# Linear attention on one core: a store that waits for the load six octets ahead through a dependency, with eight output buffers

## The chip, the cores and the metric

The kernel runs on one core of one Trainium2 chip. The metric is the device time of one execution in microseconds (us). Three runs of the kernel before the change gave 126.98, 126.65 and 126.52 us, a median of 126.65 us.

## The reference

The kernel computes linear attention with a ReLU feature map, for 8 batches of 12 heads, 512 rows of sequence and 64 columns, everything in float32 in HBM:

```python
Q_feat = np.maximum(0, Q)
K_feat = np.maximum(0, K)
KV = np.einsum('bhkd,bhkv->bhdv', K_feat, V)
K_sum = np.sum(K_feat, axis=2)
numerator = np.einsum('bhqd,bhdv->bhqv', Q_feat, KV)
denominator = np.einsum('bhqd,bhd->bhq', Q_feat, K_sum)
return numerator / (denominator[:, :, :, None] + 1e-10)
```

Q, K, V and the output have 8 x 12 x 512 x 64 float32 elements each, 12.58 MB.

## The kernel before

The 96 heads are cut into 12 **octets** of 8 heads (the variable `o`, from 0 to `NO - 1` = 11), and each octet into two **groups** of 4 heads (`g` = 2o and 2o + 1). A group of K or of V is 0.52 MB in HBM; the Q of an octet and the output of an octet are 1.05 MB each. An octet therefore reads 3.15 MB and writes 1.05 MB.

**Loads.** Only the four loads of octet 0's K and V go through the queues of SP and ACT, as float32 (lines 103 to 107). All others are issued by GpSimd (POOL) in one fixed order and turn float32 into bf16 on the way (`load_kv`, lines 94 and 96, and `load_q`, line 100): for each octet K, V, K, V, Q. They land in rings of 12 K tiles, 12 V tiles and 7 Q tiles, so loads run octets ahead of the arithmetic. POOL does nothing else of weight.

**Arithmetic.** The program order of the engines is written out by hand (a manual schedule; lines 254 to 328). For an octet, DVE and ACT apply the ReLU to K and spread K and V into block layouts (`prep` line 136 and 138, `prep_v` lines 143 and 145). PE accumulates KV in PSUM (`mm_kv`, line 150), ACT copies it out (`evac_kv`, line 160). PE transposes Q (`transp`, line 171), ACT applies the ReLU (line 179). PE forms the denominators (line 210) and the transposed outputs (line 201), ACT copies those out (line 203), PE turns them back (`back`, line 228), and DVE multiplies by the reciprocal denominators into the output tile `o_sb` (`norm`, line 234). In the main loop octet o's arithmetic goes with the conversion of octet o + 1's K and V, and the outputs of octet o - 1 are finished there (`backs(o - 1)`); the last four octets have an order of their own.

**Stores.** The output tiles come from the pool `outp` (line 51, `DELAY + 2` = 7 buffers of 8 KB per partition). Two of its buffers first hold the float32 K and V of octet 0. `store(o, o_sb)` (lines 240 to 249) issues the store of octet o on the SP queue, which executes in order. Stores are held back on purpose: for the first seven octets SP first issues a copy of 128 bytes from the first K tile of octet o + 5 into `scratch` (line 242). That copy has to wait until this K tile has landed, and the store stands behind it in the same queue. Each copy also writes the same `scratch`, so it waits for the copy before it. Stores 7 to 11 have no such copy of their own; the last store is cut in two halves.

The lines that set it:

```python
DELAY = 5
outp = pool("outp", DELAY + 2)
if o + DELAY < NO:
    nc.sync.dma_start(out=scratch, in_=k_sb[2 * (o + DELAY)][0:1, 0, :])
```

Of the kernel before, what the change touches and what calls it, by code (L numbers as in the profile page):

```python
# [10 lines left out]
def kernel(  # L11
# [7 lines left out]
    nc = tc.nc  # L19
    B, H, S, D = Q.shape  # L20
# [10 lines left out]
    NG = NH // NHG  # L31
    NO = NG // 2
    assert NO * 8 == NH and R == 16 and RQ == 32
    DELAY = 5
    F32 = 2

    fp32 = mybir.dt.float32
    bf16 = mybir.dt.bfloat16
# [3 lines left out]
    def pool(name, bufs, **kw):  # L42
        return ctx.enter_context(tc.tile_pool(name=name, bufs=bufs, **kw))

    consts = pool("consts", 1)
# [4 lines left out]
    rcp = pool("rcp", 2)  # L50
    outp = pool("outp", DELAY + 2)
    otp = pool("otp", 2)
# [5 lines left out]
    def view(X, f):  # L58
        return X.rearrange("b h s d -> (b h s d)").rearrange("(n p f) -> n p f", p=P, f=f)

    Qr, Kr, Vr, Or = view(Q, RQ * D), view(K, R * D), view(V, R * D), view(out, RQ * D)
# [14 lines left out]
    kvf = [consts.tile([P, 8 * 2 * D1], bf16, name=f"kvd{i}") for i in range(NK)]  # L76
    kvd = [x.rearrange("p (h d) -> p h d", h=8) for x in kvf]
    mask = consts.tile([P, 2, 2], fp32, name="mask")
    scratch = consts.tile([1, D], bf16, name="scratch")

    mask_h = consts.tile([P, 8, 2], fp32, name="mask_h")

# [5 lines left out]
    ctx.enter_context(tc.manual_schedule())  # L88

    q_sb, k_sb, v_sb = {}, {}, {}  # L90

    def load_kv(g):
        k_sb[g] = kin.tile([P, R, D], bf16, name="k_sb")
        nc.gpsimd.dma_start(out=k_sb[g].rearrange("p r d -> p (r d)"), in_=Kr[g])  # L94
        v_sb[g] = vin.tile([P, R, D], bf16, name="v_sb")
        nc.gpsimd.dma_start(out=v_sb[g].rearrange("p r d -> p (r d)"), in_=Vr[g])  # L96

# [12 lines left out]
    for o in range(1, NO):  # L110
        load_kv(2 * o)
        load_kv(2 * o + 1)
        load_q(o)
# [124 lines left out]


    def store(o, o_sb):  # L240
        if o + DELAY < NO:
            nc.sync.dma_start(out=scratch, in_=k_sb[2 * (o + DELAY)][0:1, 0, :])
        Ov = Or[o].rearrange("p (r d) -> p r d", d=D)
        if o == NO - 1:
            for j in range(2):
                rs = slice(RQ // 2 * j, RQ // 2 * (j + 1))
                nc.sync.dma_start(out=Ov[:, rs], in_=o_sb[:, rs])
            return
        nc.sync.dma_start(out=Ov, in_=o_sb)

    def out_tile():
        return outp.tile([P, RQ, D], fp32, name="o_sb", tag="o_sb")
# [19 lines left out]
    def backs(o):  # L272
        o_sb = out_tile()
        for j in range(2):
            norm(o, j, back(o, j), o_sb)
        store(o, o_sb)
# [26 lines left out]
    o = NO - 2  # L303
    g = 2 * NO - 2
# [9 lines left out]
    o_sb = out_tile()  # L314
# [4 lines left out]
    for i in range(2):  # L319
        relu_q(o + 1, i, transp(o + 1, i), nc.vector if i == 1 else None)  # L320
    norm(o, 1, ps, o_sb)
    store(o, o_sb)
    idle(5, o + 1)
    out_t(o + 1, (0,))
# [32 lines left out]
```

## Time and profile before

| What | Value |
|---|---|
| median of three runs | 126.65 us (126.52 to 126.98) |
| span of the profiled execution, first to last instruction | 124.8 us |
| median less span | 1.85 us |
| PE, DVE, ACT busy | 69%, 65%, 64% of the span |
| HBM read, written | 37.75 MB, 12.58 MB |
| store issue to landing, median of 11 whole stores | 9.0 us |
| K, V, Q load issue to landing, medians | 14.1, 13.2, 14.8 us |
| 128-byte copy on SP, issue to landing, median of 7 | 5.0 us |

The profile gives the span of the execution that it recorded; a time of its own for that execution, with what lies around the span, is not given. The 1.85 us between the span and the median of the runs is therefore taken as fixed here. In the profile "DMA share" is the time that packets took, over 16 engines: 1.00 and above means that each of the 16 always had a packet in hand (packets of one engine can overlap, so it can pass 1). "GB/s" counts what was moved by packet size; a converting load counts with its bf16 size, half of what it read from HBM. For loads alone the HBM rate is thus twice the number shown.

### The profile page before, as it was taken

Reading aid. Unit: us, or ns where it says so; the run is one execution under the profiler, and the core shown is the slowest. Engines: PE = TensorE matmul, PEld = TensorE weight load, DVE = VectorE, ACT = ScalarE, POOL = GpSimd, SP = SyncE. Lnnn points to the kernel's source line nnn. Section 1 sums busy time; section 2 is a strip of 40 time slices with the busy share of each in tenths; the row PEclk is TensorE's granted clock in tenths of the full one; section 3 lists DMA queues with packets and bytes.
Section 4 is the critical chain, followed back from the end, with each engine's and each line's share of the span. In section 5 each row is a group of like instructions: output and inputs, shape, how many; then the busy total and the mean of one; then the engine's idle time right before and its main releaser. Section 6 shows DMA issues by size and latency. Waiting matters only on the chain.

```text
span 124.8 us, 2656 instructions
## 1 busy us (share of the span) xinstructions
PE 86.6 (69%) x1067; PEld 78.5 (63%) x1067; DVE 81.1 (65%) x176; ACT 79.4 (64%) x114; POOL 31.2 (25%) x62
## 2 busy tenths in 40 slices
PE   0032287998889899893598599399777577797600
PEld 0031285997878787792597499299576476695500
DVE  2257644759797997989147845934928918979430
ACT  0163369989898999988149558665939737737100
POOL 6902434314243331142133115034122000000000
PEclk9999999999999999999779859959999999999995
DMA  3999999999999999999999999999999999999993
GB/s 112 377 306 215 215 205 210 217 205 218 203 215 211 206 223 324 253 216 300 281 215 280 304 213 249 331 215 230 334 234 218 323 257 215 312 421 420 428 416 143
DMA packets 10748, 32.68 MB, mean 262 GB/s; under 512 B 1392, under 2 KB 1392, under 8 KB 9328
## 3 DMA queue, kind: packets, MB, share of 16 engines
q0 software_dynamic: 8064, 17.83, 74.7%
q1 hardware_dynamic: 2384, 13.63, 27.1%
q10 hardware_dynamic: 288, 1.05, 2.2%
q8 instruction: 8, 0.13, 0.4%
q14 instruction: 4, 0.03, 0.1%
HBM read 37.75 MB, written 12.58 MB: 403 GB/s over the span
## 4 chain that ended last, share of the span: by engine, by line
DMA 34%; DVE 30%; PE 23%; ACT 5%; issue 2%; DVEq 1%; SPq 0%; POOLq 0%; ACTq 0%
DMA v_sb<-in_V_dram 14%; DVE o_sb L234 13%; DMA q_sb<-in_Q_dram 13%; PE ps_kv L150 11%; DMA kv_first<-in_K_dram 7%; PE ps_bk L228 7%; DVE kf L136 5%; PE ps_qt L171 4%; DVE vo L138 3%; ACT kvd L160 2%; DVE vo L145 2%; PE ps_ot L201 2%; DVE den L218 2%; ACT qt L179 2%; DVE rec L222 1%
## 5 line engine op out<-in xcount | busy, mean ns | idle before, releaser
L150 PE MATMUL ps_kv<-vo,kf 128*128 128x132 bf16 x384 | 30.8, 244 | 17.7 <-ACT vo L143 8.2
L150 PEld LDWEIGHTS <-kf 128*128 128x128 bf16 x384 | 28.4, 110 | 19.0 <-DVE vo L138 10.9
L234 DVE TENSOR_TENSOR o_sb<-ps_bk,rec 128x1024 f32<-128x1024 f32 x24 | 28.3, 1219 | 17.1 <-PE ps_bk L228 17.1
L160 ACT CAST kvd<-ps_kv 64x260 bf16<-64x260 f32 (+1 forms) x54 | 18.7, 346 | 19.5 <-PE ps_kv L150 16.6
L203 ACT COPY ot_sb<-ps_ot 128x1024 f32<-128x1024 f32 x24 | 24.0, 1014 | 3.0 <-PE ps_ot L201 2.0
L179 ACT ACTIVATE qt<-ps_qt 128x1024 bf16<-128x1024 bf16 x23 | 22.4, 1026 | 5.6 <-PE ps_qt L171 5.5
L228 PE MATMUL ps_bk<-ident,ot_sb 128*128 128x128 f32 x192 | 23.0, 273 | 0.4 <-ACT ot_sb L203 0.4
L136 DVE TENSOR_SCALAR kf<-k_sb,mask 128x1024 bf16<-128x1024 bf16 x44 | 18.4, 460 | 6.4 <-DMA k_sb<-in_K_dram 6.3
L94 POOL DMA_DIRECT2D k_sb<-in_K_dram x22 | 11.9, 542 | 37.7 <-DMA q_sb<-in_Q_dram 24.1
L228 PEld LDWEIGHTS ps_bk<-ident,ot_sb 128*128 128x128 f32 x192 | 20.8, 141 | 0.7 <-ACT ot_sb L203 0.7
L171 PE MATMUL ps_qt<-ident,q_sb 128*128 128x128 bf16 x192 | 16.0, 250 | 6.0 <-DMA q_sb<-in_Q_dram 5.9
L171 PEld LDWEIGHTS <-q_sb 128*128 128x128 bf16 x192 | 14.3, 114 | 7.3 <-DMA q_sb<-in_Q_dram 7.1
L201 PE MATMUL ps_ot<-qt,kvd 128*128 128x256 bf16 x96 | 14.7, 283 | 5.0 <-DVE o_sb L234 4.3
L96 POOL DMA_DIRECT2D v_sb<-in_V_dram x22 | 12.3, 558 | 17.4 <-DMA k_sb<-in_K_dram 11.1
L201 PEld LDWEIGHTS <-kvd 128*128 128x128 bf16 x96 | 9.2, 101 | 7.8 <-issue 5.7
L138 DVE TENSOR_SCALAR vo<-v_sb,mask 128x1024 bf16<-128x1024 bf16 x22 | 10.6, 482 | 1.8 <-DMA v_sb<-in_V_dram 1.8
L143 ACT ACTIVATE vo<-v_sb,mask 128x1024 bf16<-128x1024 bf16 x10 | 11.5, 1152 | 0.2
L210 PEld LDWEIGHTS <-qt 128*128 128x128 bf16 x192 | 6.8, 97 | 4.4 <-ACT qt L179 3.4
L210 PE MATMUL ps_den<-kvd,qt 128*128 128x16 bf16 x192 | 7.5, 180 | 2.4 <-ACT qt L179 2.1
L100 POOL DMA_DIRECT2D q_sb<-in_Q_dram x12 | 6.6, 546 | 8.5 <-DMA v_sb<-in_V_dram 6.2
L213 DVE SCALAR_TENSOR_TENSOR own<-ps_den,mask_h 128x256 f32<-128x256 f32 x12 | 5.0, 417 | 3.3 <-PE ps_den L210 3.3
L136 DVE TENSOR_SCALAR kf<-kv_first,mask 128x1024 bf16<-128x1024 f32 x4 | 2.8, 749 | 5.1 <-DMA kv_first<-in_K_dram 5.1
(24 smaller groups left out, 28.3 us busy)
## 6 DMA issues: line engine op xcount, KB each, us to landing
out_dram<-o_sb SPq DMA_DIRECT2D x11, 1024.0 KB, 9.0
q_sb<-in_Q_dram POOLq DMA_DIRECT2D x12, 512.0 KB, 14.8
k_sb<-in_K_dram POOLq DMA_DIRECT2D x22, 256.0 KB, 14.1
v_sb<-in_V_dram POOLq DMA_DIRECT2D x22, 256.0 KB, 13.2
kv_first<-in_V_dram ACTq DMA_DIRECT2D x2, 512.0 KB, 7.2
kv_first<-in_K_dram SPq DMA_DIRECT2D x2, 512.0 KB, 6.9
out_dram<-o_sb SPq DMA_DIRECT2D x2, 512.0 KB, 4.3
scratch<-k_sb SPq DMA_DIRECT2D x7, 0.1 KB, 5.0
```

Source lines behind the costliest of these rows:

```text
L96: nc.gpsimd.dma_start(out=v_sb[g].rearrange("p r d -> p (r d)"), in_=Vr[g])
L136: nc.vector.tensor_scalar(kf[g][:, :, s, :], k_sb[g], scalar1=0.0, scalar2=mask[:, 0, s:s + 1], op0=Alu.max, op1=Alu.mult)
L138: nc.vector.tensor_scalar(vo[g % NB][:, :, 0, 2:D + 2], v_sb[g], scalar1=mask[:, 1, 0:1], scalar2=None, op0=Alu.mult)
L150: nc.tensor.matmul(ps_kv[:, g % 2, 0:2 * (D + 2)].rearrange("p (t d) -> p t d", t=2), kf[g][:, r, :, :].rearrange("p s d -> p (s d)"), vo[ ...
L160: copy(kvd[o % NK][64 * c:64 * c + 64, 4 * gs.start + s:4 * gs.stop:2, c * D1:c * D1 + D1].rearrange("p (g t) d -> p g t d", t=2), ps_kv[6 ...
L171: nc.tensor.transpose(ps[:, u, :], q_sb[o][:, i * (U // 2) + u, :], ident)
L179: nc.scalar.activation(to, ps, Act.Relu)
L201: nc.tensor.matmul(ps[:, i], kvd[o % NK][:, h, 1:2 * D + 1], q[:, :, h, :], start=True, stop=True, skip_group_check=True)
L203: nc.scalar.copy(ot[o][:, :, 4 * j:4 * j + 4], ps.rearrange("p h u c -> p u h c"))
L210: nc.tensor.matmul(ps[:, u], qt_sb[o % NZ][:, u, :], kvd[o % NK][:, :, 0:2 * D1:2 * D1 - 1], start=True, stop=True, skip_group_check=True)
L228: nc.tensor.transpose(ps[:, 2 * v:2 * v + 2].rearrange("p c d -> p (c d)"), ot[o][:, 8 * j + v].rearrange("p h c -> p (h c)"), ident32)
L234: nc.vector.tensor_tensor(o_sb[:, rs], ps, rec[o][:, rs].unsqueeze(2).to_broadcast([P, 16, D]), op=Alu.mult)
```

## The change

`DELAY` goes from 5 to 6, so the pool of output tiles has 8 buffers instead of 7, and the stores of octets 0 to 5 (before: 0 to 6) wait for the first K tile of the octet six later. The 128-byte copy and its `scratch` tile are gone. Instead `load_kv` keeps the instruction of each octet's first K load, and the store gets a dependency on that instruction. Order of loads, arithmetic and stores is the same.

```diff
-    DELAY = 5
+    DELAY = 6
...
-    scratch = consts.tile([1, D], bf16, name="scratch")
...
+    k_load = {}
+    after_load = mybir.DependencyInfo(mybir.DependencyClass.Sync, mybir.DependencyReason.DATA)
 
     def load_kv(g):
         k_sb[g] = kin.tile([P, R, D], bf16, name="k_sb")
-        nc.gpsimd.dma_start(out=k_sb[g].rearrange("p r d -> p (r d)"), in_=Kr[g])
+        ld = nc.gpsimd.dma_start(out=k_sb[g].rearrange("p r d -> p (r d)"), in_=Kr[g])
+        if g % 2 == 0:
+            k_load[g // 2] = ld
...
     def store(o, o_sb):
-        if o + DELAY < NO:
-            nc.sync.dma_start(out=scratch, in_=k_sb[2 * (o + DELAY)][0:1, 0, :])
         Ov = Or[o].rearrange("p (r d) -> p r d", d=D)
...
-        nc.sync.dma_start(out=Ov, in_=o_sb)
+        st = nc.sync.dma_start(out=Ov, in_=o_sb)
+        if o + DELAY < NO:
+            tc.add_manual_dep(st.ins, k_load[o + DELAY].ins.name, after_load, reason="store after load")
```

## The prediction

> **What bounds the kernel now.** I read the page's slices over time first, with the queue table under them, because the engines are busy only 64 to 69% of the span and the DMA row is not.
>
> ```profile
> DMA  3999999999999999999999999999999999999993
> GB/s 112 377 306 215 215 205 210 217 205 218 203 215 211 206 223 324 253 216 300 281 215 280 304 213 249 331 215 230 334 234 218 323 257 215 312 421 420 428 416 143
> ...
> q0 software_dynamic: 8064, 17.83, 74.7%
> q1 hardware_dynamic: 2384, 13.63, 27.1%
> ...
> HBM read 37.75 MB, written 12.58 MB: 403 GB/s over the span
> ```
>
> The DMA digit is 9 in every slice but the first and the last. Second view: the busy time by stretches, cut where the kind of traffic changes (loads alone to 42.85; loads with one store per octet to 102.85; then the tail; the last two columns are DMA share and GB/s).
>
> ```profile
> 12.00:42.85 30.85, 25.07 (x316) 22.94 (x317) 22.27 (x51) 24.78 (x39) 10.95 (x20) 1.00 1.10 210
> 42.85:102.85 60.00, 47.08 (x585) 42.95 (x585) 40.37 (x80) 42.12 (x59) 14.41 (x27) 0.91 1.09 263
> 102.85:110.00 7.15, 5.63 (x69) 5.04 (x67) 6.52 (x14) 5.31 (x10) 0.00 (x0) 1.00 1.09 279
> 110.00:118.00 8.00, 6.85 (x86) 5.79 (x84) 5.53 (x10) 3.59 (x5) 0.00 (x0) 1.00 1.01 424
> 118.00:122.00 4.00, 0.05 (x1) 0.00 (x0) 1.57 (x2) 0.00 (x0) 0.00 (x0) 1.00 1.00 415
> 122.00:123.60 1.60, 0.00 (x0) 0.00 (x0) 0.00 (x0) 0.00 (x0) 0.00 (x0) 0.59 0.51 207
> ```
>
> The share is 1.00 or more from 12 to 122 us: no DMA engine runs out of packets there. From 110 only stores move. The last 1.6 us are a drain at half share, and then about 1.2 us of closing waits end the span. Third view: SP's timeline, which shows the gate.
>
> ```profile
> 82.87 0.50 SPq L242 DMA_DIRECT2D scratch<-k_sb  x1
> ...
> 92.86 0.50 SPq L242 DMA_DIRECT2D scratch<-k_sb  x1
> 93.46 0.53 SPq L249 DMA_DIRECT2D out_dram<-o_sb  x1
> 102.85 0.50 SPq L242 DMA_DIRECT2D scratch<-k_sb  x1
> 103.45 11.23 SPq L249 DMA_DIRECT2D out_dram<-o_sb  x5
> 118.47 1.46 SPq L247 DMA_DIRECT2D out_dram<-o_sb  x2
> ```
>
> The gates open 10.0 us apart (42.90, 52.89, 62.89, 72.92, 82.87, 92.86, 102.85). One such period moves 3.15 MB of loads and 1.05 MB of store: 4.19 MB / 10.0 us = 419 GB/s. Loads alone run at 2 x 210 = 420 GB/s of HBM reads, stores alone at 424. So the three kinds of traffic cost the same per byte, and 50.3 MB / 0.42 = 119.8 us, which with some 3 us before the first data flow is the end of the transfers at 122 to 123.6. Last I read the chain of waits, which seems to say something else: its tail is arithmetic.
>
> ```profile
> 116.09 1.11 PE ps_bk L228 x8
> 117.19 0.02 issue
> 117.22 1.22 DVE o_sb L234
> 118.44 1.13 DVEq L352
> ```
>
> The chain follows engines and semaphores, and cannot see that a transfer queues behind older bytes. The two half stores issued at 118.47 and 119.6 land after 4.2 to 4.3 us. Half a megabyte at 0.42 MB/us takes 1.25 us; share 1.00 up to 122 says that the rest is at least partly queue. Both things end here almost together: the arithmetic hands over its last tile about when the queue of earlier stores has run down, and the bytes set the end.
>
> **The change part by part.**
>
> *One more store moves behind the loads.* Store 0 was released by octet 5's K (42.9). Octet 6's K landed at 52.89, with one store mixed in; without it an octet's loads take 3.15 / 0.420 = 7.5 us, so I expect the first gate at 42.9 + 7.5 = 50.4, then every 10.0 us, and the sixth and last (octet 11's K) at 100.4 instead of 102.85. All later loads come 2.5 us sooner, and store 6 joins the tail: after the last gate six whole stores and the two halves remain instead of five and the halves.
>
> *What the transfers' end does.* Bytes are the same. The moved store costs 10.0 - 7.49 = 2.51 us in the mixed phase and 1.05 / 0.424 = 2.47 us in the store phase: a gain of 0.04 us. Bounds: the slices with stores alone run from 416 to 428 GB/s, which makes the moved store 2.45 to 2.52 us, a gain of 0.06 or a loss of 0.01; I take 0.04, from the longest stretch.
>
> *What the arithmetic does.* It waited for loads in the middle: PE for Q at 60.77 (2.9 us), DVE for K at 62.90 (3.0 us) and 72.92 (1.65 us). With loads 2.5 us sooner these waits stay or just vanish, so the arithmetic's last multiply should move from 118.44 to about 116. Its price on the end is nothing, because the stores ahead of it in the queue then number one more: 2.5 us sooner in, 2.5 us more ahead. The cover is the store queue. If it were gone, the end would be issue plus service: 1.25 us for the data and what a lone transfer pays besides.
>
> *The drain.* In 122.0 to 123.6 the share is 0.51, so 0.49 x 1.6 = 0.78 us of 16 engines is lost. If that is starvation (the last halves arriving a little late at an almost empty queue), a longer queue regains up to 0.78 us. If the 16 engines just end their equal parts at unequal times, it regains nothing. The row nearest to it, 118 to 122 at share 1.00 with the first half issued at 118.47, shows no starvation, so I take 0 and keep 0.78 for the range.
>
> *The copies on SP.* Seven issues of 0.50 to 0.59 us go from SP. They lie in waits of up to 41 us, so they cost nothing; a store now starts 0.6 us sooner after its gate, again into a full queue. As transfers they are 7 x 128 bytes, under 0.001 MB. The wait for the copy before (24.9 us in total, six times) always ended before K came, since copies land in 5.0 us and gates are 10 us apart.
>
> *The wait on SP.* SP carries only stores after the first loads, so behind the waiting store 5 stand stores 6 to 11, and nobody waits for these but the closing waits and the output buffers. With 8 buffers, two of which hold octet 0's K and V first, octet 8 takes the buffer of store 0: landed by 50.4 + 13.2 (the longest landing) = 63.6, wanted after 90. For octets 9, 10 and 11 the distance stays above 20 us. POOL's queue is untouched: its loads are paced by older loads (24.1 us of waits on Q landings), and the rings of K, V and Q tiles are as before. One more store is outstanding after the last gate (5, 6, 7 and 8 at once and 9 soon after, instead of 6, 7, 8 and then 9 at 105.8); it could at worst block SP's issue, behind a queue that is full anyway.
>
> Sum: -0.04 + 0 + 0 = no change that can be measured; 126.65 - 0.04 rounds to 126.6. The profiled span of 124.8 should stay 124.8 (the 1.85 us around it fixed).
>
> A page against the trace: the 0.42 MB/us here stand above the per-core limit of about 358 GB/s that the Trainium skill gives in "DMA: Bandwidth & Descriptors", Specifications; by that figure alone 50.3 MB would need 141 us, more than the whole run, so here the measurement decides. The same table's fabric ceiling of 435 GB/s would put the transfers at an estimated 115.7 us, 4 us less than the 119.8 above; that would speak for a gain from any change that packs them better, but here loads alone, stores alone and both mixed stand at 420, 424 and 419, so I see nothing that this change packs. [...]
>
> **The rivals.**
>
> *A (forecast): the bytes set the end.* 126.6; own range 126.1 to 127.1.
>
> *B: the drain is starvation.* For it: the arithmetic hands over its last half at 119.6, with the queue nearly run down. Against: full share until 122. A deeper queue saves up to 0.78 us: 125.9. Faster by 0.6%.
>
> *C: the chain is right, the last tile sets the end.* Then the whole 2.5 us come off: 124.1 to 124.5. Against: for a store that has not been moved before the last load, its bytes are still to be moved after it, and the share of 1.00 leaves no hole to put them in; C needs engines that move 1.05 MB more than 420 GB/s allow.
>
> *D: the dependency is fulfilled by the issue of the K load and not its landing.* This is the case in which the change doesn't do what it says. Octet 6's K was issued at 38.25 and octet 11's at 85.90, so stores 0 to 8 would all be out when their tiles are ready (store 8's at about 97), three more than the six before 102.85. Three stores at 2.5 us push the last Q from 110 or a little before to 117.5; from the Q transposes (110.98) to the last multiply's end took 7.46 us, so 125, and a half store behind an empty queue 1.25 to 4.3 us more. End of landing 126.3 to 129.3 against 123.8: 129 to 132 us in all, 130.6 in the middle. It decides from where the last Q lands more than about 1 us later than before. For it: nothing in this trace shows how such an edge is turned into a wait. Against: an ordinary dependency on a K load makes DVE's conversion wait for the landing (6.3 us, three times, released by the DMA of K).
>
> **How the numbers follow.** Under 0.5%, 0.63 us, counts as no change for this kernel. A 0.78, B 0.11, C 0.03, D 0.05; 0.03 for slowdowns that I can't name. Faster: B and C, 0.14. Slower: 0.08. Same: 0.78. A holds 126.1 to 127.1 with most of its weight; to leave out no more than 2 in 10 the range goes down to B's full gain (125.8) and up to 127.2.
>
> **What would show it.** SP without copies, stores released near 50.4, 60.4, 70.4, 80.4, 90.4 and 100.4; a last multiply near 116; four stores issued one after the other from 100.4, a fifth near 103.3; DMA share 1.00 up to about 122, and store traffic alone from about 107.5. B is right if the drain becomes shorter than 1 us. D is right if the first store goes out at about 38. I am wrong if the rate of the stores alone falls with six queued, or if the share drops anywhere before 120.

## The result, and the profile after

The changed kernel takes 127.07 us (median of 8 runs, 126.93 to 127.15), the kernel before 126.68 us (8 runs, 126.52 to 126.98): a ratio of 1.0029, 95% interval 1.0019 to 1.0040. That is slower by 0.37 us, less than the 0.5% that I called no change, but clearly not zero, and I had forecast zero or a shade less. The profiled execution took 127.14 us with a span of 125.3 us; so 1.8 us lie around the span, as I had assumed, and the loss is inside it (124.8 before).

The first view is the page of the changed kernel, its slices and the queue of the stores:

```profile
DMA  3999999999999999999999999999999999999992
GB/s 101 380 305 215 216 207 211 214 207 217 210 209 210 209 218 204 216 305 277 212 286 301 210 259 329 209 236 333 228 218 324 256 212 317 400 424 429 424 405 86
...
q1 hardware_dynamic: 2160, 13.63, 26.7%
```

Queue q1 has the same bytes and 224 packets fewer: the 128-byte copies. The second view is its busy time by stretches, cut at the new gates (last two columns: DMA share and GB/s):

```profile
42.85:50.40 7.55, 6.79 (x100) 6.28 (x98) 6.60 (x15) 6.97 (x10) 2.71 (x5) 1.00 1.10 211
50.40:100.40 50.00, 37.73 (x466) 34.42 (x464) 32.36 (x63) 33.03 (x47) 12.03 (x22) 0.90 1.08 262
100.40:107.50 7.10, 5.58 (x73) 4.98 (x71) 5.57 (x11) 5.53 (x10) 0.00 (x0) 1.00 1.08 282
107.50:118.00 10.50, 7.86 (x95) 6.74 (x92) 8.03 (x13) 4.21 (x8) 0.00 (x0) 1.00 1.01 421
118.00:122.00 4.00, 0.00 (x0) 0.00 (x0) 0.03 (x1) 0.00 (x0) 0.00 (x0) 0.77 1.00 415
122.00:124.00 2.00, 0.00 (x0) 0.00 (x0) 0.00 (x0) 0.00 (x0) 0.00 (x0) 0.50 0.42 170
```

There is one more stretch of loads alone (to 50.4), then almost only stores from 107.5 (the last Q lands at 109.2), a full share to 122, and a drain as long as before. The third view is SP's timeline of the changed kernel, the first line of its stores and the two halves of the last:

```profile
50.41 62.72 SPq L250 DMA_DIRECT2D out_dram<-o_sb  x11
116.93 1.46 SPq L248 DMA_DIRECT2D out_dram<-o_sb  x2
```

The first gate at 50.4 and transfers that end where they did are what I forecast; the last store is issued 1.5 us sooner, where I had forecast about 2.5. The half stores land 5.8 to 5.9 us after issue instead of 4.2 to 4.3, so the last lands at 118.06 + 5.9 = 124.0 against 119.60 + 4.3 = 123.9.

What I had not looked at comes after the landing. At the end of the program SP goes through the program's semaphores in a fixed order, one instruction after the other. These are the instructions of that closing line, first of the kernel before in the window from 123.90 to 124.03 us, and then of the changed kernel in the window from 123.90 to 124.53 (duration min/median/max in ns, first and last start in us):

```profile
L352 SPq EVENT_SEMAPHORE  x1: 28/28/28, 123.9 to 123.9; - x1
L352 SPq DRAIN  x1: 7/7/7, 124.0 to 124.0; - x1
```

```profile
L355 SPq EVENT_SEMAPHORE  x8: 28/28/28, 124.0 to 124.4; - x8
L355 SPq DRAIN  x1: 7/7/7, 124.5 to 124.5; - x1
```

Before, one check follows the last landing. After, eight do. The waits of SP in the closing stretch (from 118 us on) say the same from the other side: before, SP is stopped three times, once by each of the last three stores; in the changed kernel once, for 5.5 us, because the second check in its order already belongs to the store that lands last. (The three numbers are the total wait in us, how often, and the longest.)

```profile
SPq L352 <- DMA out_dram<-o_sb: 3.5, 3, 1.2
```

```profile
SPq L355 <- DMA out_dram<-o_sb: 5.5, 1, 5.5
```

The operands in the trace give the reason. The transfers of the SP and ACT queues take eight completion semaphores in turn; in both kernels these are 107, 109, 111, 112, 115, 116, 117 and 118, and SP's closing checks go through them in that order. Before there are 24 such transfers (4 first loads, 7 copies, 11 stores, 2 halves), so the last one takes the eighth, 118. Without the copies there are 17, and the last one takes the first, 107. The seven checks behind it start 61 ns apart (124.013 to 124.442 us, 0.429 / 7), which is 0.43 us. The span grew by 125.34 - 124.82 = 0.52 us: 0.43 of checks and 0.09 of a later landing. The 0.09 says little, since single profiles differ by more: in the experiments below, the last landing lies between 123.8 (the dependency on the V load) and 124.2 (the first experiment) in kernels whose transfers are all but the same.

### The profile page after: what moved, and what is told of

It reads as the page before. It is cut to its first block, busy times and chain, and to the rows that moved or that the text cites. A ratio compares the mean times of both kernels' runs of the same rounds, so it can differ in the third digit from the quotient of the medians.

```text
span 125.3 us, 2648 instructions
## 1 busy us (share of the span) xinstructions
PE 84.3 (67%) x1067; PEld 76.8 (61%) x1067; DVE 80.9 (65%) x176; ACT 79.1 (63%) x114; POOL 31.3 (25%) x62
## 3 DMA queue, kind: packets, MB, share of 16 engines
q10 hardware_dynamic: 288, 1.05, 2.2%
## 4 chain that ended last, share of the span: by engine, by line
DMA 32%; DVE 31%; PE 21%; ACT 5%; issue 2%; DVEq 1%; SPq 0%; ACTq 0%; POOLq 0%
DMA q_sb<-in_Q_dram 14%; DVE o_sb L237 13%; DMA v_sb<-in_V_dram 12%; PE ps_kv L153 11%; DMA kv_first<-in_K_dram 7%; PE ps_bk L231 7%; DVE kf L139 5%; ACT kvd L163 3%; DVE vo L141 3%; PE ps_qt L174 3%; DVE vo L148 2%; DVE den L221 2%; DVE rec L225 2%; DVE own L216 2%; ACT qt L182 2%
## 5 line engine op out<-in xcount | busy, mean ns | idle before, releaser
L153 PE MATMUL ps_kv<-vo,kf 128*128 128x132 bf16 x384 | 29.8, 239 | 18.0 <-ACT vo L146 8.2
L153 PEld LDWEIGHTS <-kf 128*128 128x128 bf16 x384 | 27.3, 107 | 19.4 <-DVE vo L141 11.0
L95 POOL DMA_DIRECT2D k_sb<-in_K_dram x22 | 11.8, 536 | 40.1 <-DMA q_sb<-in_Q_dram 18.1
L204 PE MATMUL ps_ot<-qt,kvd 128*128 128x256 bf16 x96 | 13.9, 271 | 5.0 <-DVE o_sb L237 4.3
```

The lines of the kernel that those rows point to most:

```text
L153: nc.tensor.matmul(ps_kv[:, g % 2, 0:2 * (D + 2)].rearrange("p (t d) -> p t d", t=2), kf[g][:, r, :, :].rearrange("p s d -> p (s d)"), vo[ ...
L204: nc.tensor.matmul(ps[:, i], kvd[o % NK][:, h, 1:2 * D + 1], q[:, :, h, :], start=True, stop=True, skip_group_check=True)
```

## The experiments

Every kernel ran beside the kernel before on the same chip; "checks" below means the closing checks from the one that waits for the last landing to the last one.

**The changed kernel with the last store on the eighth semaphore.** Seven small copies right behind octet 0's loads use up seven semaphores and do nothing else:

```diff
+    spare = consts.tile([1, 8, D], fp32, name="spare")
...
+    for i in range(7):
+        nc.sync.dma_start(out=spare[:, i, :], in_=Kr[0][0:1, 0:D])
     load_q(0)
```

> The changed kernel with seven copies of 256 bytes (from K in HBM to a spare tile) issued on SP right behind octet 0's loads. They do nothing but use up seven completion semaphores, so that the last half store signals semaphore 118 again, the last of the eight store semaphores that SP's closing waits go through, and not 107, the first. Theory S (order of the closing waits): in the changed kernel eight checks of about 61 ns follow the landing where before there was one, so this kernel should come back by 7 x 61 ns = 0.43 us: 126.6 to 126.7 us, ratio to before 0.998 to 1.001, landing to the last check in one step. Rival T (the store moved into the tail makes the transfers end later): nothing comes back, 127.0 to 127.1, ratio 1.003. Rival U (the missing copies or the dependency itself): also 127.0 to 127.1.

Measured: 126.75 us, ratio 0.9996 (0.9982 to 1.0010). The loss is gone, although the stores, the gate and the dependency are those of the changed kernel. (The eighth semaphore has the number 117 in this kernel, because 118 serves the engines here; the order of the checks is as before.) SP's waits in the closing stretch are three again:

```profile
SPq L358 <- DMA out_dram<-o_sb: 4.1, 3, 1.7
```

**The kernel before with the last store on the first semaphore.** One such copy in the kernel before (`range(1)`):

> The kernel before with one copy of 256 bytes on SP behind octet 0's loads and nothing else changed: DELAY 5, copies from K, 7 output buffers. It moves the last half store from semaphore 118 to 107. Theory S: slower by 0.43 us, ratio 1.0034 (1.002 to 1.0045), with seven more checks after the landing. Rivals T and U: the same as before, ratio 0.999 to 1.001, since neither the stores nor the way of waiting change.

Measured: 127.40 us, ratio 1.0049 (1.0035 to 1.0062). A copy of 256 bytes in the first two microseconds makes the old kernel as slow as the changed one or slower. The ratio lies above the range that I expected, and its interval only overlaps it: some 0.2 us more than seven checks cost. In its profile the last store also landed 0.2 us later than before (124.1 against 123.9), but so it did in the profile of the kernel above, whose time is not longer; the cause of these 0.2 us stays open. SP is stopped once here, as in the changed kernel:

```profile
SPq L355 <- DMA out_dram<-o_sb: 4.6, 1, 4.6
```

**A dose: three small copies in the changed kernel** (`range(3)`), five checks:

> The changed kernel with three spare copies instead of seven, so that the last half store signals 112, the fourth of the eight. Theory S gives a dose: five checks from the landing on instead of eight, three fewer by 61 ns = 0.18 us off the changed kernel, 126.85 to 126.95, ratio about 1.0015 to 1.002. Rival T and U: 127.0 to 127.1, ratio 1.003.

Measured: 126.96 us, ratio 1.0020 (1.0011 to 1.0028), between the two ends as theory S says, though the interval still overlaps that of the changed kernel. SP is stopped four times, and the fourth stop is the first of the last five checks:

```profile
SPq L358 <- DMA out_dram<-o_sb: 5.3, 4, 2.4
```

**DELAY 6 and eight buffers alone, in the kernel before with its copies kept:**

```diff
-    DELAY = 5
+    DELAY = 6
```

> DELAY 6 and 8 output buffers alone: the kernel before with its copies from K kept, six of them now, so 23 transfers on the SP and ACT queues and the last half store on semaphore 117, with two checks from the landing on instead of one. Theory S (order of the closing waits, the bytes set the rest): slower by one check, 0.06 us, ratio 1.0000 to 1.0015. If the store moved into the tail costs something of its own: 1.003 or more.

Measured: 126.76 us, ratio 0.9999 (0.9990 to 1.0008). Moving the store into the tail costs nothing. Four kernels whose arithmetic is ahead of the transfers now give ratios of 0.9996, 0.9999, 1.0020 and 1.0029 for 1, 2, 5 and 8 checks: from first to last 0.0033 x 126.7 us / 7 = 60 ns a check (the intervals allow 30 to 90), against 61 ns in the trace.

**The dependency alone**, the changed kernel with the old DELAY:

```diff
-    DELAY = 6
+    DELAY = 5
```

> The dependency alone: the changed kernel with DELAY 5 and 7 output buffers. There are 17 transfers on the SP and ACT queues as in the changed kernel, so the last half store signals 107. Theory S: as slow as the changed kernel, ratio 1.002 to 1.004. Rival T: as fast as before, ratio 0.999 to 1.001, since stores go out at the times of before. Rival U: as slow as the changed kernel.

Measured: 128.36 us, ratio 1.0111 (1.0070 to 1.0151), its executions between 127.2 and 128.85. That is a miss: a second cost of about 1 us that the closing order doesn't explain. A second set of runs of the same kernel was to show whether this comes back:

> The dependency alone once more, DELAY 5, 7 buffers. Its executions lay between 127.2 and 128.85 us. Theory E (late Q loads and a queue that runs empty) expects the same spread, and in a profile of a slow one the last multiply ends at 120.5 or later, with DMA engines idle before 122. Theory that the spread was that chip's: 127.0 to 127.2 in all.

It gave 127.76 us, ratio 1.0086 (1.0065 to 1.0106). Its profiled execution (127.89 us) shows where the time goes. First the stretches of the kernel before from 118 us on, then those of this run:

```profile
118.00:120.00 2.00, 0.05 (x1) 0.00 (x0) 1.57 (x2) 0.00 (x0) 0.00 (x0) 1.00 1.00 420
120.00:122.00 2.00, 0.00 (x0) 0.00 (x0) 0.00 (x0) 0.00 (x0) 0.00 (x0) 1.00 1.00 410
122.00:124.00 2.00, 0.00 (x0) 0.00 (x0) 0.00 (x0) 0.00 (x0) 0.00 (x0) 0.57 0.41 166
```

```profile
118.00:120.00 2.00, 1.50 (x14) 1.26 (x12) 1.34 (x2) 0.00 (x0) 0.00 (x0) 1.00 0.98 414
120.00:122.00 2.00, 0.00 (x0) 0.00 (x0) 1.02 (x1) 0.00 (x0) 0.00 (x0) 1.00 0.82 340
122.00:124.00 2.00, 0.00 (x0) 0.00 (x0) 0.00 (x0) 0.00 (x0) 0.00 (x0) 1.00 0.76 301
```

The last multiply still runs until 121.02 us, and the DMA share falls to 0.82 (0.55 in the first half microsecond after 120) before the last half store comes at 121.05: here the queue does run empty, and the last tile sets the end. The last half lands at 124.76 instead of 123.91; these 0.85 us and the 0.43 us of checks are the 1.27 us by which the span is longer (126.09 against 124.82). This is my rival C, in a kernel that I had not thought of. The issue lines of the page give the first link, Q's median time to landing, first before and then in the first run of this kernel (the second has the same):

```profile
q_sb<-in_Q_dram POOLq DMA_DIRECT2D x12, 512.0 KB, 14.8
```

```profile
q_sb<-in_Q_dram POOLq DMA_DIRECT2D x12, 512.0 KB, 15.8
```

The second link is when the stores start, again before and in that first run, from SP's timeline:

```profile
43.53 0.57 SPq L249 DMA_DIRECT2D out_dram<-o_sb  x1
```

```profile
42.79 72.71 SPq L250 DMA_DIRECT2D out_dram<-o_sb  x11
```

Without the copy ahead of it the first store is issued at 42.79 instead of 43.53, the one after the last gate at 103.0 instead of 103.45, so 0.4 to 0.7 us sooner, and the Q load under way beside each store ends later. The last Q lands 17.0 us after its issue at 94.8, at 111.8, where before it took 16.0 us from 94.7, to 110.7. Why single executions of this kernel differ by up to 1.6 us is not shown.

**The same dependency on the V load, which lands 1.25 us after K:**

```diff
-    DELAY = 6
+    DELAY = 5
...
-        ld = nc.gpsimd.dma_start(out=k_sb[g].rearrange("p r d -> p (r d)"), in_=Kr[g])
-        if g % 2 == 0:
-            k_load[g // 2] = ld
+        nc.gpsimd.dma_start(out=k_sb[g].rearrange("p r d -> p (r d)"), in_=Kr[g])
         v_sb[g] = vin.tile([P, R, D], bf16, name="v_sb")
-        nc.gpsimd.dma_start(out=v_sb[g].rearrange("p r d -> p (r d)"), in_=Vr[g])
+        ld = nc.gpsimd.dma_start(out=v_sb[g].rearrange("p r d -> p (r d)"), in_=Vr[g])
+        if g % 2 == 0:
+            k_load[g // 2] = ld
```

> The dependency with DELAY 5 and 7 buffers as in the run with the dependency alone, but on the V load that lands some 1.25 us after the K load. Theory E (without the copy a store starts 0.6 us sooner, its bytes go ahead of the next Q load, which lands 1 us later; the arithmetic then hands over its last halves 0.8 us later, to a queue that has run empty): stores wait 0.7 us longer than before, Q lands as early as before or earlier, and only the closing order is left: 127.0 to 127.2, ratio 1.002 to 1.0045, last multiply's end near 119. Rival F (a wait on a load inside the store is itself what costs the extra 1.3 us): as slow as the run on K, ratio 1.008 to 1.014.

Measured: 127.11 us, ratio 1.0033 (1.0020 to 1.0046): the closing order and no more, though the store waits by a dependency as before. Its first store goes out at 44.11, and Q's median is back:

```profile
q_sb<-in_Q_dram POOLq DMA_DIRECT2D x12, 512.0 KB, 14.7
```

So rival F falls and theory E stands: the issue time of the store, not the way of waiting, costs the second microsecond.

**The dependency alone with the last store on the eighth semaphore** (DELAY 5 and `range(7)`):

> The dependency alone with DELAY 5 and 7 buffers, and seven spare copies behind octet 0's loads so that the last half store signals 118. If the two costs of that run are separate, the closing order (0.43 us) goes and the late Q loads (some 1 us and more in most executions) stay: ratio 1.004 to 1.010, 127.2 to 128. If the whole excess came from the closing order or from a disturbed chip: ratio 0.998 to 1.002.

Measured: 127.14 us, ratio 1.0047 (1.0027 to 1.0068), executions from 126.75 to 128.27. Against the two runs without the small copies (1.0111 and 1.0086) the closing order is gone (its profile has one check after the last landing), and a rest stays: the two costs are separate. How large the rest is varies between the sets of runs, 0.6 to 1.0 us.

**The changed kernel without a gate** (the dependency left out, seven small copies):

> The changed kernel without any gate: no dependency on a load, stores go out when their tile is ready; seven spare copies keep the last half store on 118. If the bytes set the end in every order: 126.6 to 126.8, ratio 0.998 to 1.002. If the gate is what keeps the arithmetic off the end: eight or nine stores go ahead of the last loads instead of five, the last Q lands near 115 to 117 instead of 109.2, the last multiply ends near 123 to 125, and the time is 129 to 132 us, ratio 1.02 to 1.04, with DMA engines idle in the last 5 us.

Measured: 133.48 us, ratio 1.0537 (1.0504 to 1.0570), more than I expected. The last Q lands at 117.9, and the DMA engines have next to nothing to do for 4 us (the run's stretches):

```profile
118.00:122.00 4.00, 3.30 (x52) 2.80 (x50) 3.21 (x7) 2.50 (x4) 0.00 (x0) 1.00 0.12 49
122.00:126.00 4.00, 2.72 (x23) 2.15 (x21) 2.32 (x4) 1.08 (x2) 0.00 (x0) 1.00 0.63 262
```

Against 126.75 us with the gate and the same small copies, the gate is worth 6.7 us. It keeps enough stores back to fill the time of the last octet's arithmetic; the bytes set the end only behind such a gate.

**Towards a faster kernel: the last store in one piece** (16 transfers, so the eighth semaphore without any spare copy), with the gate at six, eight and ten octets ahead, always 8 buffers (shown for ten; with six only the last part changes):

```diff
-    DELAY = 6
+    DELAY = 10
...
-    outp = pool("outp", DELAY + 2)
+    outp = pool("outp", 8)
...
-        if o == NO - 1:
-            for j in range(2):
-                rs = slice(RQ // 2 * j, RQ // 2 * (j + 1))
-                nc.sync.dma_start(out=Ov[:, rs], in_=o_sb[:, rs])
-            return
```

> The changed kernel with the last store in one piece: 16 transfers on the SP and ACT queues, so that the last one signals 118 without any spare copy. Theory S: back by 0.43 us, 126.55 to 126.7, ratio 0.998 to 1.000; the whole store is issued when the second multiply is done, near 118, behind a queue that lasts to about 121.5. If a last store in one piece costs more than a check saves, that is, if the queue runs out before it: 127.0 or more.

> The changed kernel with the last store in one piece (118) and the gate eight octets ahead instead of six; still 8 buffers, so four stores wait and eight are left for the tail. If the bytes set the end as soon as the arithmetic is far enough ahead: the same as with six, 126.5 to 126.75, ratio 0.998 to 1.0005, with the last multiply some 3 to 5 us sooner. If more stores in the tail cost: above 1.002. If a longer queue packs the drain: below 0.997.

> As the kernel with the gate eight octets ahead and the last store in one piece, but ten octets ahead, still 8 buffers: two stores wait, ten go in the tail. If each store that leaves the mixed phase saves a little (two fewer gave about 0.1 to 0.2 us): 126.3 to 126.5, ratio 0.996 to 0.998. If the gain of the gate at eight was only the last piece of store queued deeper: the same as there, 0.997 to 0.999. The tile of octet 9 now waits for store 1, released near 90; if that stall comes through to the end, above 1.000.

Measured: six ahead 126.71 us, ratio 0.9991 (0.9982 to 1.0000); eight ahead 126.49 us, 0.9978 (0.9968 to 0.9989); ten ahead 126.31 us, 0.9958 (0.9941 to 0.9974). The last beats both kernels, and its page says why there is little more to get: loads alone until about 80, then stores among and behind the last loads, and no slice in which the rate falls off before the end.

```profile
GB/s 105 391 303 211 216 205 209 217 206 218 204 213 210 209 221 203 216 207 209 216 206 219 204 209 217 205 233 325 244 214 318 402 429 427 424 419 422 429 427 145
```

The tile of octet 9 does wait for a store there, as expected, and the wait is paid out of time that the arithmetic has to spare (DVE's waits in this run; the last multiply still ends at 116.6):

```profile
DVE o_sb L237 <- DMA out_dram<-o_sb: 8.9, 1, 8.9
```

From six to ten ahead, four stores leave the mixed phase and the time falls by 0.0033 x 126.7 = 0.42 us, some 0.1 us a store (the intervals allow 0.05 to 0.16). The trace agrees in size: an octet of loads alone takes 7.45 us in the last kernel (Q landings at 64.0 and 78.9, two octets apart) and one with a store 10.0 us (88.9 and 98.9), so a store costs 2.55 us among loads and 2.47 us among stores. The drain has no part in it: the last three stores land 2.46 and 2.44 us apart with ten ahead and 2.43 and 2.42 with six.

## Why the prediction was right or wrong

- *What bounds the kernel: the bytes.* Right. Share 1.00 to 122 us in both kernels, the last landing 0.09 us apart with the last store issued 1.5 us sooner, and ratios of 0.9991 to 0.9999 with one or two checks.
- *The step that failed: the copies on SP, costed at nothing, and with them the 1.2 us of closing waits that I read off the profile and carried over as fixed.* I counted the copies' issue time, bytes and waits, and not that each takes a completion semaphore in turn. Taking seven away moved the last store from the eighth to the first of eight, and seven checks of 61 ns went behind the landing: 0.43 us, shown by moving the semaphore alone in both kernels.
- *A second fault of the same step: "a store now starts 0.6 us sooner after its gate, again into a full queue".* The time is right (0.4 to 0.7 us), the cost isn't nothing: it delays each Q by about 1 us. With DELAY 5 that alone would have made the kernel 0.5 to 0.8% slower. In the changed kernel the additional octet of loads ahead covers it: the last Q came 1.5 us sooner (109.2 against 110.7) and not 2.5 us (with DELAY 6 and the copies kept it lands at 108.5, 16.0 us after its issue instead of 17.0), and the last multiply began at 115.67 + 1.23 = 116.90 against 118.44, where I had forecast about 116.
- *One more store behind the loads, 0.04 us.* Right in sign, too small: some 0.1 us a store in the last series. I took the rate of loads alone from a stretch with a slower patch (7.49 us an octet against 7.45; Q landed at 18.1 and then at 27.0) and one store alone can't show it beside 0.43 us.
- *The half store's landing as partly queue.* Supported: in the two runs with the dependency alone, where the halves met a nearly empty queue, they took 3.1 to 3.7 us, against 4.2 to 4.3 before and 5.8 to 5.9 in the changed kernel, where more lay ahead of them. The Trainium skill ("DMA: Bandwidth & Descriptors", "Anatomy of one DMA") gives its fit of about 2.0 us plus the bytes at 436 GB/s for transfers that GpSimd issues, an estimated 3.2 us for half a megabyte. The half stores are issued by SP, so that figure does not speak of them, though the 3.1 to 3.7 us lie near it.
- *The drain.* Right to take 0: a queue longer by 1.5 us left it at 0.42 of 2 us, against 0.51 of 1.6 before (0.84 and 0.82 us of work).
- *The wait on SP, the buffers, POOL.* No multiply waited for an output buffer in the changed kernel, and SP's waits for K held up nothing but the stores, as forecast.
- *Rivals.* B and C did not happen in the changed kernel; C did in the kernel with the dependency alone. D fell at the first gate (50.4, with octet 6's K landed at 50.3): the dependency waits for the landing. D's price was also short: 118.44 is where the last multiply begins and not where it ends, and the kernel without a gate, with the last Q at 117.9 as D had it (117.5), took 133.48 us and not 129 to 132. "Slowdowns that I can't name" had 0.03; it was one of these, though below the 0.5%; that chance named no mechanism.

The sum as it should have been, put together afterwards: 0.43 for the checks, about 0.1 less for the moved store, 0.33 us; measured 0.37 (0.24 to 0.51).

## What to carry to other kernels

When a change adds or removes transfers, however small, count them: the last transfer's place in the turn of completion semaphores, and the order in which the program's end checks them, are worth up to 0.43 us here, and one idle copy at the start moves them. In a kernel that the bytes bound, ask how long the queue of bytes still is when the last result is handed over: before the change it was an estimated microsecond (4.3 us to landing against 3.1 to 3.7 on a nearly empty queue), enough to hide everything, and stores issued half a microsecond too soon used it up. Stores held back until the loads are through gain about 0.1 us each here, as long as the output buffers last.

## What the runs showed of the hardware that I had not expected

A closing check that finds its semaphore already set still takes 61 ns, one after the other (seven of them in 0.43 us). A store of 1.05 MB issued some half a microsecond sooner makes a load that was issued 8 us before it (Q at 94.8, the store at 103.0) land 1.0 us later: here a store is not served behind the loads that other queues were given first.
